# A two-layer decoder trunk on one core: the first conditioning pair on TensorE, later pairs in quarter steps, the gates token-major, the second phase split from its third k-tile on

## The chip, the core and the metric

The kernel runs on one core of one Trainium2 chip. The time is device microseconds for one execution, and the number compared is the median of several executions. TensorE (PE), VectorE (DVE), ScalarE (ACT) and the DMA queue of SyncE (SP) each work through a list of their own, in the order of that list, and wait for each other through semaphores. GpSimd (POOL) only clears a few tiles here.

## What is computed

One sequence of 256 tokens (T) and width 2048 (D, so 16 k-tiles of 128, KT) goes through two layers. All that the change touches lies at the very start of layer 0, before the first half of the mixer is done. Cut to that:

```python
mod = silu(c) @ ada_w[0] + ada_b[0]            # (12288): shift, scale, gate of two sub-layers
h = rms_norm(x, norm1_g[0]) * (1 + scale) + shift
p = h @ w_in                                    # 2048 x 8200
qk_m, v_m, o_m, if_m, q_r, k_r, v_r, g_r = split(p)
gates = 15 * tanh((if_m + gate_b) / 15)         # 8 columns: 4 input gates, 4 forget gates
log_i, log_f = gates[:, :4], log_sigmoid(gates[:, 4:])
# mLSTM: exp(dmat - running max) of cumulated gates weights the 256 x 256 scores of each of 4 heads
```

All data is float32. Most products are made in three float32r passes: weight and activation are each split into a rounded high part and a rest, and high x high, high x rest and rest x high are added.

## The kernel before

The normalised input is turned to feature-major, `xT` (16 tiles of 128 x 256). To become `h`, each k-tile needs its shift and its scale, which are sums over 2048 conditioning inputs. They are made in eight pairs (`pr` 0 to 7, two k-tiles each). A pair reads 4.19 MB of `ada_w` as four quarter tiles `ar` (ring of four). VectorE multiplies and adds 16 slices into `acc0`, which is the fold (L752, L754). `row_sums` turns the accumulator on TensorE (L332) and sums it on ScalarE (L335). Two small VectorE operations give `mod` and `acol` (L765, L767), ScalarE makes `hf` (L772), and `split_to_hs` makes the high part and the rest (L206, L207).

Three phases of the input projection run while the pairs are made, because the weights can't be used before the pair is there:

- First phase (`nb`, `q0b`): k-tiles 0 to 3 (`PART`), for the values and the first query columns, in plain float32 from `raw` (`wplain`, or straight in the loop).
- Second phase (`gbs`, `vbs`): k-tiles 0 to 7 (`HALF`), for the output gate and the last values, in plain float32.
- Third phase (`qk = sums(7)`): all 16 k-tiles for 14 column tiles of queries and keys. K-tiles 0 to 5 are in plain float32 from `hf`; the rest is split. `wload` fetches into `raw`; ScalarE rounds to `wh` (L232), VectorE subtracts to `wl` (L234), and `nmul2` issues three matmuls for each column tile.

After the third phase comes the rest of the first phase's columns (k-tiles 4 to 15, all split), called the V phase here. It reuses the seven PSUM banks of the third phase, so ScalarE first copies them out (`qkr`).

`gates()` stands in the program at k-tile 8 of the third phase. It computes the 8 gate columns with `tmul`, feature-major (8 x 256), turns them, forms cumulated sums, a running maximum over 256 positions in eight doubling steps on VectorE (L899, L900), and four 128 x 384 matrices `E`. All of it uses PSUM bank 3 alone, because the seven others hold the third phase.

A fourth thing runs alongside: `Fill`, which folds 512 KB rows of `ada_w` (tile `ada`, L400, L402) for later sub-layers, two to a k-tile from k-tile 12 on.

The order on each engine is set by a scheduler that takes the program in written order with priorities; the splits carry a raised priority. Slots of the rings (`raw`, `wh`, `wl` of four, `ada` of three, `ar` of four) decide when a transfer may be issued, and SP issues transfers strictly in its order.

Of the kernel before, what the change touches and what calls it, by code (L numbers as in the profile page):

```python
# [94 lines left out]
def tile_trunk(ctx: ExitStack, tc: tile.TileContext, io, out):  # L95
# [522 lines left out]
    def mlp(l, before, fill, norm):  # L618
        with ExitStack() as es:
# [33 lines left out]
            if l == 1:  # L653
# [4 lines left out]
                zp.tile([P, 24], F32, name="pad")  # L658
# [32 lines left out]
    with ExitStack() as es:  # L691
# [24 lines left out]
        early = [load_ar(0, 0), load_ar(0, 1)]  # L716
# [25 lines left out]
        sums_of = {}  # L742

        def cond_sum(pr):

            acc = sums_of[pr] = sp0.tile([P, 2, T], F32, tag="acc0", bufs=3, name="acc0")
            for kq in range(4):
                ar = early.pop(0) if early else load_ar(pr, kq)
                for kr in range(4):
                    cc = cond[:, kq * 4 + kr:kq * 4 + kr + 1]  # L750
                    if kq == 0 and kr == 0:
                        V.tensor_scalar(acc, ar[:, kr], cc, None, op0=OP.mult)  # L752
                    else:
                        V.scalar_tensor_tensor(acc, ar[:, kr], cc, acc, op0=OP.mult, op1=OP.add)  # L754

        def cond_pair(pr):

            if pr not in sums_of:
                cond_sum(pr)
            acc = sums_of.pop(pr)  # L760
            cs = st(4, "adac")
            row_sums(cs, [acc[:, i // 2, (i % 2) * P:(i % 2 + 1) * P] for i in range(4)])
            two_k = slice(2 * pr, 2 * pr + 2)
            mview = mod[0][:, 0:32].rearrange("p (c k) -> p c k", c=2)[:, :, two_k]
            V.tensor_tensor(mview, cs.rearrange("p (c k) -> p c k", c=2),  # L765
                            bada[0][:, 0:32].rearrange("p (c k) -> p c k", c=2)[:, :, two_k], op=OP.add)
            V.scalar_tensor_tensor(acol[:, 0, 0, two_k], mod[0][:, 16 + 2 * pr:18 + 2 * pr], 1.0,  # L767
                                   ngain[0, 0][:, two_k], op0=OP.add, op1=OP.mult)
            out = {}
            for k in (2 * pr, 2 * pr + 1):  # L770
                hf = sp0.tile([P, T], F32, tag="hf", bufs=8, name="hf") if k < HALF else tmp.tile([P, T], F32, tag="half", name="half")
                S.activation(hf, xT[:, k, :], AF.Identity, scale=acol[:, 0, 0, k:k + 1], bias=shift(0, 0)[:, k:k + 1])  # L772
                hs[k] = split_to_hs(hf)
                out[k] = hf
            return out
# [18 lines left out]
        hfs = {}  # L794
        for pr in range(PART // 2):
            ws = {}
            hfs.update(cond_pair(pr))
# [23 lines left out]
        def load_c(k):  # L821
            wc[k] = wplain(k, 3072, 4096), wplain(k, 6664, 7176)

        for k in range(PART):
            load_c(k)
            if k % 2 == 1:
                cond_sum((PART + k - 1) // 2)
        for k in range(HALF):
# [4 lines left out]
            for j in range(8):  # L833
                mm(gbs[j // 2][:, j % 2 * T:j % 2 * T + T], wa[:, j * P:(j + 1) * P], hfs[k], a and j % 2 == 0, z)
            for t in range(2):
                mm(vbs[t], hfs[k][:, t * P:(t + 1) * P], wb[:, 0:512], a, z)
            if k % 2 == 1 and k < PART:
                hfs.update(cond_pair((PART + k - 1) // 2))
            elif k % 2 == 1:
                cond_sum((PART + k - 1) // 2)  # L840
# [12 lines left out]
        c1 = sp0.tile([P, c1w], F32, name="c1")  # L853
# [541 lines left out]
```

## Time and profile before

| | |
|---|---|
| median of 3 runs | 2344.75 us (2341.22 to 2345.06) |
| profiled execution | 2340.88 us |
| its span, first to last instruction | 2339.1 us |
| PE, DVE, ACT busy | 97%, 73%, 51% of the span |
| HBM read | 607 MB, 261 GB/s over the span |

TensorE's idle time is nearly all in the first tenth of the span, and the change is made there. The profile's timeline of one engine gives, for merged instructions, their start, the time that they took together, and in brackets the idle time before them with what ended it. Its groups by shape give the busy time, the mean of one instruction in ns, and the idle time before them.

### The profile page before, as it was taken

The numbers are of one execution on the slowest core, as the hardware profiler recorded it, in microseconds if no ns is written. First come the engines' busy times: TensorE is split into PE (matmuls) and PEld (weight loads), VectorE is DVE, ScalarE is ACT, GpSimd is POOL, SyncE is SP. The second block draws the span as 40 slices with busy tenths as digits, with TensorE's granted clock in tenths as the row PEclk, the third lists the DMA queues.
The fourth block names the chain that finished last, engine by engine and source line by source line (L and its number), as shares of the span: only waits on it lengthen the run. The fifth ranks groups of instructions, "written<-read, shape, count | busy, mean of one in ns | idle before, by whom it ended". The sixth has DMA issues, their size and how long they took to land.

```text
span 2339.1 us, 37507 instructions
## 1 busy us (share of the span) xinstructions
PE 2280.5 (97%) x14121; PEld 2033.0 (87%) x14121; DVE 1704.9 (73%) x2499; ACT 1191.6 (51%) x2248; POOL 0.5 (0%) x8
## 2 busy tenths in 40 slices
PE   5899998999999999999999999999999999999999
PEld 3689888999988888999989899999988888888887
DVE  5768897995877777888988779865777455555555
ACT  3225455455555556655555445664655555444443
POOL 0000000000000000000000000000000000000000
PEclk8999999999999999999999999999999999999999
DMA  9998998996699999999899787645798665555554
GB/s 329 355 300 285 297 319 286 326 325 207 215 311 318 317 316 315 310 305 315 284 327 320 233 271 229 227 139 176 242 313 269 182 188 188 189 198 192 193 191 162
DMA packets 268909, 611.97 MB, mean 262 GB/s; under 512 B 26692, under 2 KB 95286, under 8 KB 268728
## 3 DMA queue, kind: packets, MB, share of 16 engines
q1 hardware_dynamic: 268728, 609.59, 78.2%
q8 instruction: 110, 1.80, 0.3%
q14 instruction: 71, 0.58, 0.1%
HBM read 607.38 MB, written 2.12 MB: 261 GB/s over the span
## 4 chain that ended last, share of the span: by engine, by line
PE 80%; DVE 9%; DMA 6%; issue 2%; ACT 2%; SPq 0%; DVEq 0%; ACTq 0%
PE L L124 49%; PE M L124 30%; DMA ada<-in_ada_w_dram 3%; DVE wl L234 3%; DMA raw<-in_even_w_in_dram 2%; DVE acc L402 1%; DVE acc L754 1%; PE M L332 1%; ACT wh L232 1%; DMA raw<-in_mlp_w_dram 1%; ACT junk L335 0%; DVE cv L1064 0%; DVE hs L207 0%; SPq L243 0%; PE M L737 0%
## 5 line engine op out<-in xcount | busy, mean ns | idle before, releaser
L234 DVE TENSOR_TENSOR wl<-raw,wh 128x1024 fp32r<-128x1024 f32 (+1 forms) x724 | 876.7, 1213 | 489.4 <-ACT wh L232 480.1
L232 ACT CAST wh<-raw 128x1024 fp32r<-128x1024 f32 (+1 forms) x724 | 753.7, 1042 | 830.6 <-PE M L124 442.1
L124 PE MATMUL L<-hs,wh 128*128 128x256 f32 (+1 forms) x4608 | 1131.7, 324 | 6.5 <-ACT wh L232 4.2
L124 PE MATMUL L<-hs,wl 128*128 128x256 f32 x3120 | 874.8, 281 | 2.4 <-DVE wl L234 2.4
L124 PEld LDWEIGHTS L<-hs,wh 128*128 128x128 f32 x4608 | 772.1, 190 | 70.9 <-ACT wh L232 5.9
L124 PEld LDWEIGHTS L<-hs,wl 128*128 128x128 f32 x3120 | 591.0, 190 | 4.1 <-DVE wl L234 3.2
L124 PE MATMUL M<-hs,wh 128*128 128x512 f32 (+2 forms) x1816 | 518.6, 347 | 0.0
L402 DVE SCALAR_TENSOR_TENSOR acc<-ada,cond,acc 128x1024 f32<-128x1024 f32 x300 | 383.3, 1278 | 30.5 <-DMA ada<-in_ada_w_dram 30.0
L124 PE MATMUL M<-hs,wl 128*128 128x256 f32 (+2 forms) x1444 | 403.1, 279 | 0.0
L124 PEld LDWEIGHTS M<-hs,wh 128*128 128x128 f32 (+1 forms) x1816 | 313.7, 187 | 52.1 <-issue 1.6
L124 PEld LDWEIGHTS M<-hs,wl 128*128 128x128 f32 (+2 forms) x1444 | 269.2, 186 | 1.9 <-issue 1.0
L124 PE MATMUL L<-wh,zh 128*128 128x512 f32 x512 | 168.7, 389 | 0.0
L124 PE MATMUL M<-wh,zh 128*128 128x512 f32 x512 | 168.6, 389 | 0.0
L124 PEld LDWEIGHTS L<-wh,zh 128*128 128x128 f32 x512 | 96.0, 188 | 20.2 <-issue 0.3
L124 PEld LDWEIGHTS M<-wh,zh 128*128 128x128 f32 x512 | 96.2, 188 | 20.0
L335 ACT ACTIVATE junk<-M 128x128 f32<-128x128 f32 x210 | 55.2, 278 | 88.0 <-PE M L332 87.9
L124 PE MATMUL L<-wl,zh 128*128 128x512 f32 x256 | 99.7, 389 | 0.0
L124 PE MATMUL M<-wl,zh 128*128 128x512 f32 x256 | 99.6, 389 | 0.0
L754 DVE SCALAR_TENSOR_TENSOR acc<-ar,cond,acc 128x512 f32<-128x512 f32 x120 | 90.2, 751 | 4.8 <-DMA ar<-in_ada_w_dram 1.0
L634 ACT ACTIVATE half<-half 128x256 f32<-128x256 f32 x120 | 47.8, 411 | 28.6 <-DVE half L325 28.6
L124 PE MATMUL L<-hf,raw 128*128 128x256 f32 x224 | 53.3, 392 | 4.9 <-DMA raw<-in_even_w_in_dram 4.9
L124 PEld LDWEIGHTS L<-wl,zh 128*128 128x128 f32 x256 | 48.1, 188 | 10.2 <-DVE wl L234 0.3
(273 smaller groups left out, 1575.4 us busy)
## 6 DMA issues: line engine op xcount, KB each, us to landing
raw<-in_mlp_w_dram SPq DMA_DIRECT2D x504, 512.0 KB, 4.6
ada<-in_ada_w_dram SPq DMA_DIRECT2D x320, 512.0 KB, 5.3
raw<-in_even_w_in_dram SPq DMA_DIRECT2D x136, 256.0 KB, 5.4
ar<-in_ada_w_dram SPq DMA_DIRECT2D x64, 512.0 KB, 7.8
raw<-in_odd_w_in_dram SPq DMA_DIRECT2D x48, 512.0 KB, 4.5
raw<-in_even_w_out_dram SPq DMA_DIRECT2D x32, 512.0 KB, 5.3
raw<-in_odd_w_out_dram SPq DMA_DIRECT2D x32, 512.0 KB, 4.2
raw<-in_even_w_in_dram SPq DMA_DIRECT2D x28, 512.0 KB, 6.1
```

Source lines behind the costliest of these rows:

```text
L124: PE.matmul(o, a, b, start=start, stop=stop, skip_group_check=True)
L232: S.copy(wh[:, :n], raw[:, :n])
L234: last_split[0] = V.tensor_tensor(wl[:, :n], raw[:, :n], wh[:, :n].bitcast(F32), op=OP.subtract)
L332: PE.transpose(b[:, i * P:(i + 1) * P], t, ident)
L335: S.activation(j, b[:, i * P:(i + 1) * P], func, accum_out=dst[:, i:i + 1])
L402: V.scalar_tensor_tensor(acc, r, cond[:, kr:kr + 1], acc, op0=OP.mult, op1=OP.add)
L634: S.activation(a, a, AF.Relu)
L754: V.scalar_tensor_tensor(acc, ar[:, kr], cc, acc, op0=OP.mult, op1=OP.add)
```

## The change

The change has five parts.

1. All four quarter tiles of pair 0 are requested ahead of the small parameter rows. The pair's 16 slices are multiplied on TensorE: the stationary operand is one column of `cond` repeated 32 times (`cond32`), and slice `kr` of each quarter goes to rows 32 x `kr` of a bank. ScalarE copies the bank out, and a column `quad` that has a one in every 32nd row adds the four strips.
2. For every pair, `row_sums` is replaced by four matmuls with `acc` stationary and one column moving; `mod` reads their result in PSUM.
3. `conditioned()` is a generator: the loops of the phases take it forward by quarters of a pair (`cond_steps`) and no longer by whole pairs.
4. The second phase is split from k-tile 2 on, the third from k-tile 4 on.
5. `gates()` is token-major, 64 small float32r matmuls with the activations stationary and 8 or 16 gate columns moving. It is a generator too, begun at k-tile 8 and taken forward by small steps inside the matmul loop from k-tile 12 on. Its constants `c1` now lie in `xT`, and a padding tile shrinks from 24 to 16 columns.

```diff
-        early = [load_ar(0, 0), load_ar(0, 1)]
+        early = [load_ar(0, kq) for kq in range(4)]
...
+        quad = small.tile([P, 1], F32, tag="quad", bufs=1, name="quad")
+        V.reduce_sum(quad, c0[:, 0:128:32], axis=AX.X)
...
+        def cond32(k):
+            return bass.AP(tensor=cond.tensor, offset=cond.offset + k, ap=[list(cond.ap[0]), [0, 32]])
...
+        def conditioned():
+            for pr in range(KT // 2):
+                acc = sp0.tile([P, 2, T], F32, tag="acc0", bufs=3, name="acc0")
+                if pr == 0:
+                    b = bank(3)
+                for kq in range(4):
+                    ar = early.pop(0) if early else load_ar(pr, kq)
+                    for kr in range(4):
+                        cc = cond[:, kq * 4 + kr:kq * 4 + kr + 1]
+                        if pr == 0:
+                            mm(b[32 * kr:32 * kr + 32, :], cond32(kq * 4 + kr),
+                               ar[:, kr].rearrange("p c t -> p (c t)"), kq == 0, kq == 3)
+                        elif kq == 0 and kr == 0:
+                            V.tensor_scalar(acc, ar[:, kr], cc, None, op0=OP.mult)
+                        else:
+                            V.scalar_tensor_tensor(acc, ar[:, kr], cc, acc, op0=OP.mult, op1=OP.add)
+                    if kq < 3:
+                        yield
+                if pr == 0:
+                    S.copy(acc.rearrange("p c t -> p (c t)"), b)
+                cs = bank(3)[:, 0:4]
+                for i in range(4):
+                    mm(cs[:, i:i + 1], acc[:, i // 2, (i % 2) * P:(i % 2 + 1) * P], one1 if pr else quad, i == 0, i == 3)
...
         def load_c(k):
-            wc[k] = wplain(k, 3072, 4096), wplain(k, 6664, 7176)
+            if k < 2:
+                wc[k] = wplain(k, 3072, 4096), wplain(k, 6664, 7176)
+            else:
+                wc[k] = wload(wE, k, 1, [(3072, 4096)]), wload(wE, k, 1, [(6664, 7176)])
...
+                    nmul2(j % 2)(gbs[j // 2], hs[k], *wa, j * P, P, False, z)
...
             if k == 8:
-                SP.dma_start(c1, io["c1"])
-                gates()
+                gsteps = gates()
+                next(gsteps)
...
-                if k < 6:
+                if k < 4:
                     w = wplain(k, c, c + 896)
...
+                    if k >= 12 and j in (2, 5):
+                        next(gsteps, None)
+            cond_steps(2 if k % 3 == 2 else 1)
```

What this does to the lists of the engines shows at three places. In them `acc_N` is the accumulator of a pair, `M` is a bank of the second PSUM pool (numbers tell one use from another), `L` is a bank of the first.

VectorE where the second phase begins, before: the folds of pair 1 (`acc_301`), the pair's end, then pair 2 (`acc_403`) in one piece.

```order
L754 SCALAR_TENSOR_TENSOR acc_301<-ar,cond,acc_301 128x512 x15
L765 TENSOR_TENSOR mod_83<-adac,prm 128x2x2
L767 SCALAR_TENSOR_TENSOR acol<-mod_83,prm 128x2
L207 TENSOR_TENSOR hs<-hf,hs 128x256 x2
L752 TENSOR_SCALAR acc_403<-ar,cond 128x512
L754 SCALAR_TENSOR_TENSOR acc_403<-ar,cond,acc_403 128x512 x15
```

The same place now, with pair 2 as `acc_389`, pair 3 as `acc_469`.

```order
L767 SCALAR_TENSOR_TENSOR acc_389<-ar,cond,acc_389 128x512 x3
L234 TENSOR_TENSOR wl<-raw,wh 128x1024
L234 TENSOR_TENSOR wl<-raw,wh 128x512
L767 SCALAR_TENSOR_TENSOR acc_389<-ar,cond,acc_389 128x512 x4
L234 TENSOR_TENSOR wl<-raw,wh 128x1024
L234 TENSOR_TENSOR wl<-raw,wh 128x512
L767 SCALAR_TENSOR_TENSOR acc_389<-ar,cond,acc_389 128x512 x8
L765 TENSOR_SCALAR acc_469<-ar,cond 128x512
```

Two k-tiles' splits for the second phase now stand between the quarters of pair 2.

ScalarE at the same place now (`v` and `q` are copies out of the first phase's banks; before, no `wh` stood there).

```order
L689 COPY v_220<-L_228 128x2x256
L689 COPY v_222<-L_229 128x2x256
L232 CAST wh_399<-raw_397 128x1024
L232 CAST wh_405<-raw_403 128x512
L689 COPY v_222<-L_230 128x2x256
L689 COPY v_224<-M0_231 128x2x256
```

The first of these splits, which VectorE's `wl` needs, stands behind three copies that wait for the end of the first phase.

TensorE at one of the four matrices `E` (`M3_1163<-mt` is the first), before: in the midst of k-tile 13 and 14 of the third phase.

```order
L124 MATMUL M2_690<-hs_898,wh_1443 128x256
L124 MATMUL M3_1163<-mt_1140,c1_683 128x256
L124 MATMUL M2_690<-hs_898,wh_1443 128x256
L124 MATMUL M2_690<-hs_898,wl_1444 128x256
L124 MATMUL L_684<-hs_903,wh_1476 128x256 x2
L124 MATMUL L_684<-hs_903,wl_1477 128x256
L124 MATMUL L_684<-hs_903,wh_1476 128x256 x2
```

The same matmuls now (`M2_767` is the last column tile of the third phase, `L_1863` the first bank of the V phase).

```order
L124 MATMUL M2_767<-hs_1461,wh_1817 128x256 x2
L124 MATMUL M2_767<-hs_1461,wl_1818 128x256
L124 MATMUL M3_1719<-mt_1659,xT_82 128x256
L124 MATMUL M3_1744<-mt_1659,xT_82 128x256
L124 MATMUL M3_1760<-mt_1659,xT_82 128x256
L124 MATMUL M3_1791<-mt_1659,xT_82 128x256
L953 MATMUL M3_1807<-c0_78,mt_1659 128x4
L124 MATMUL L_1863<-wh_1872,hs_451 128x512
```

All four now stand between the last matmul of the third phase and the first of the V phase, each into the same bank.

VectorE at that place now (`E<-xT,M_...` are the subtractions that empty the bank).

```order
L935 TENSOR_TENSOR mt<-mt 4x192
L234 TENSOR_TENSOR wl<-raw,wh 128x768
L934 COPY mt<-mt 4x128
L935 TENSOR_TENSOR mt<-mt 4x128
L402 SCALAR_TENSOR_TENSOR acc<-ada,cond,acc 128x1024
L945 TENSOR_TENSOR E<-xT,M_1719 128x256
L946 TENSOR_TENSOR E<-xT,M_1719 128x128
L402 SCALAR_TENSOR_TENSOR acc<-ada,cond,acc 128x1024
L945 TENSOR_TENSOR E<-xT,M_1744 128x256
L946 TENSOR_TENSOR E<-xT,M_1744 128x128
L234 TENSOR_TENSOR wl<-raw,wh 128x1024
L945 TENSOR_TENSOR E<-xT,M_1760 128x256
```

Between the pairs of subtractions stands each time a fold or a split for later work. From the output projection of this mixer on, the lists of all engines are the same as before.

## Rows read from the trace of the kernel before

**Rows 1.** Waits of TensorE, 0 to 220 us: total us, times, longest us.

```profile
PE M L332 <- DVE acc L754: 8.7, 3, 4.6
...
PE L L124 <- DMA raw<-in_even_w_in_dram: 4.9, 2, 4.6
PE L L124 <- ACT hf L772: 4.5, 2, 2.3
```

**Rows 2.** Timeline of TensorE at the phases: start us, us, count, idle before.

```profile
50.13 5.40 PE L124 MATMUL L<-raw,hf 128*128 128x512 f32 x8 [2.26 <-ACT hf L772]
...
57.94 3.60 PE L124 MATMUL L<-raw,hf 128*128 128x512 f32 x8
...
63.95 3.62 PE L124 MATMUL L<-hf,raw 128*128 128x256 f32 x16
...
69.12 3.62 PE L124 MATMUL L<-hf,raw 128*128 128x256 f32 x16
...
109.50 0.60 PE L332 MATMUL M<-c,acc 128*128 128x128 f32 x4
...
158.22 0.40 PE L124 MATMUL M<-hs,wh 128*128 128x256 f32 x2
...
158.58 0.40 PE L124 MATMUL M<-hs,wh 128*128 128x256 f32 x2
...
220.86 0.40 PE L124 MATMUL L<-wh,hs 128*128 128x512 f32 x1
```

**Rows 3.** Timeline of TensorE at small matmuls, in two places.

```profile
185.39 0.73 PE L124 MATMUL M<-lfc,c 128*128 128x4 f32 x6
185.98 0.36 PE L124 MATMUL M<-hs,wl 128*128 128x256 f32 x1
...
1367.14 0.92 PE L124 MATMUL M<-ik,iq 64*128 64x256 f32 x8
1367.99 0.50 PE L124 MATMUL L<-hs,wh 128*128 128x256 f32 x2
```

**Rows 4.** Timeline of VectorE at folds: pair 1, and two waits for transfers.

```profile
34.22 0.48 DVE L752 TENSOR_SCALAR acc<-ar,cond 128x512 f32<-128x512 f32 x1
34.73 11.78 DVE L754 SCALAR_TENSOR_TENSOR acc<-ar,cond,acc 128x512 f32<-128x512 f32 x15
...
53.97 0.49 DVE L752 TENSOR_SCALAR acc<-ar,cond 128x512 f32<-128x512 f32 x1 [2.32 <-DMA ar<-in_ada_w_dram]
...
130.18 0.49 DVE L752 TENSOR_SCALAR acc<-ar,cond 128x512 f32<-128x512 f32 x1 [11.35 <-DMA ar<-in_ada_w_dram]
```

**Rows 5.** Transfers, 10 to 130 us: total.

```profile
DMA packets 32831, 42.22 MB, mean 352 GB/s; under 512 B 1547, under 2 KB 28217, under 8 KB 32825
```

**Rows 6.** VectorE's groups by shape, 0 to 221 us: busy us, mean ns, idle before.

```profile
L234 DVE TENSOR_TENSOR wl<-raw,wh 128x896 fp32r<-128x896 f32 x20 | 21.7, 1084 | 7.3 <-ACT wh L232 7.1 <-PE M L124 0.2
L402 DVE SCALAR_TENSOR_TENSOR acc<-ada,cond,acc 128x1024 f32<-128x1024 f32 x11 | 14.1, 1278 | 4.0 <-DMA ada<-in_ada_w_dram 3.8
...
L207 DVE TENSOR_TENSOR hs<-half,hs 128x256 fp32r<-128x256 f32 x8 | 3.1, 421 | 0.2 <-ACT hs L206 0.2
...
L234 DVE TENSOR_TENSOR wl<-raw,wh 128x1024 fp32r<-128x1024 f32 x2 | 2.4, 1217 | 0.0
L912 DVE TENSOR_TENSOR E<-c,M 128x256 f32<-128x256 f32 x4 | 1.7, 420 | 1.0 <-PE M L124 0.9
...
L913 DVE TENSOR_TENSOR E<-c,M 128x128 f32<-128x128 f32 x4 | 1.1, 280 | 0.0
L234 DVE TENSOR_TENSOR wl<-raw,wh 128x768 fp32r<-128x768 f32 x1 | 0.9, 948 | 0.0
...
L900 DVE TENSOR_TENSOR mt<-mt 4x248 f32<-4x248 f32 x1 | 0.4, 397 | 0.0
```

**Rows 7.** ScalarE's groups by shape, 0 to 221 us.

```profile
L689 ACT COPY v<-L 128x512 f32<-128x512 f32 x4 | 2.3, 586 | 8.7 <-PE L L124 8.7
```

**Rows 8.** Waits of SP's queue, 0 to 220 us: total us, times, longest us.

```profile
SPq L243 <- DVE wl L234: 17.5, 10, 3.3
```

More of the change, by code (lines that the diff above doesn't have):

```diff
@@ L657, in mlp @@
                 place[0] = 0
-                zp.tile([P, 24], F32, name="pad")
+                zp.tile([P, 16], F32, name="pad")
                 result(io["mlp_w2"][l],
@@ L740, in tile_trunk @@
         free[:] = [3]
[L742 to L775, printed above, removed]
+        def cond32(k):
+            return bass.AP(tensor=cond.tensor, offset=cond.offset + k, ap=[list(cond.ap[0]), [0, 32]])
@@ new lines, in tile_trunk @@
+        hfs = {}
+        def conditioned():
[21 more added lines that the diff above has]
+                    mm(cs[:, i:i + 1], acc[:, i // 2, (i % 2) * P:(i % 2 + 1) * P], one1 if pr else quad, i == 0, i == 3)
+                two_k = slice(2 * pr, 2 * pr + 2)
+                mview = mod[0][:, 0:32].rearrange("p (c k) -> p c k", c=2)[:, :, two_k]
+                V.tensor_tensor(mview, cs.rearrange("p (c k) -> p c k", c=2),
+                                bada[0][:, 0:32].rearrange("p (c k) -> p c k", c=2)[:, :, two_k], op=OP.add)
+                V.scalar_tensor_tensor(acol[:, 0, 0, two_k], mod[0][:, 16 + 2 * pr:18 + 2 * pr], 1.0,
+                                       ngain[0, 0][:, two_k], op0=OP.add, op1=OP.mult)
+                for k in (2 * pr, 2 * pr + 1):
+                    hf = sp0.tile([P, T], F32, tag="hf", bufs=8, name="hf") if k < HALF else tmp.tile([P, T], F32, tag="half", name="half")
+                    S.activation(hf, xT[:, k, :], AF.Identity, scale=acol[:, 0, 0, k:k + 1], bias=shift(0, 0)[:, k:k + 1])
+                    hs[k] = split_to_hs(hf)
+                    hfs[k] = hf
+                yield
@@ L778, in tile_trunk, with cond_steps @@
+        steps = conditioned()
+        def cond_steps(n):
+            for _ in range(n):
+                next(steps, None)
         HALF = KT // 2
@@ L902, in gates @@
                 d *= 2
-            b = bank()
-            for t in range(2):
-                PE.transpose(b[:, t * 4:t * 4 + 4], m0[:, t * P:(t + 1) * P], ident[0:4, 0:4])
-            V.tensor_tensor(expm.rearrange("p a b -> p (a b)"), b[:, 0:8], bc.rearrange("p a b -> p (a b)"), op=OP.add)
-            S.activation(expm, expm, AF.Exp, scale=-1.0)
+            yield
+            yield
+            yield
             for h in range(4):
@@ L916, in gates @@
                 emat.append(E)
+                yield
+            b = bank()
+            for t in range(2):
+                PE.transpose(b[:, t * 4:t * 4 + 4], m0[:, t * P:(t + 1) * P], ident[0:4, 0:4])
+            V.tensor_tensor(expm.rearrange("p a b -> p (a b)"), b[:, 0:8], bc.rearrange("p a b -> p (a b)"), op=OP.add)
+            S.activation(expm, expm, AF.Exp, scale=-1.0)
         qk = sums(7)
```

74 lines of the change are left out of this document (44 added, 30 removed).

## The prediction

> **What bounds the kernel now.** I first read TensorE's waits up to the V phase. They show who releases it: folds on VectorE, 8.7 us in three waits, the transfers of weights, 4.9 us, and the activation `hf` at a pair's end, 4.5 us [rows 1]. So the start is a chain of conditioning pairs: transfer, fold, pair's end, next k-tile. TensorE's timeline then gives the phases: k-tile 2 of the first phase starts at 50.13, the second phase at 63.95, its last matmul ends near 109.5, and the V phase starts at 220.86 [rows 2]. From there on the lists change little and later not at all, so I forecast the start of the V phase and carry the difference to the end.
>
> Two rates rule the start. Transfers: VectorE waits for an `ar` quarter at 53.97 and at 130.18 [rows 4]. By then the code has asked for 17.0 and 44.0 MB (x and constants 2.3; a pair 4.19, a quarter 1.05; a k-tile of the three phases 0.92, 0.79, 0.92). That is 0.354 MB per us between the two, and the DMA view has 352 GB/s [rows 5]; so a quarter lands at about 5.5 us + MB / 0.352. VectorE: 15 folds take 11.78 us, 0.785 each, so a quarter costs 3.1 and a pair 12.3 [rows 4].
>
> **The change part by part.**
>
> *Less TensorE work.* A plain k-tile of the first phase takes 6.0 us (57.94 to 63.95) and one of the third has as many columns; one of the second takes 5.2 (63.95 to 69.12) [rows 2]. A split column tile of 256 takes 0.36 us (158.22 to 158.58) [rows 2], so a split k-tile takes 14 x 0.36 = 5.0 us in the third phase and 12 x 0.36 = 4.3 in the second. Six k-tiles save 0.9 and two save 1.0: 7 us. Against that stand the gates: 64 small matmuls with a 128-column weight. The nearest row, six of four columns in 0.59 us (185.39 to 185.98) [rows 3], gives 0.1 each, 6.4 us; that is about as much as the 32 wider ones that they replace need, and TensorE waits for VectorE there anyway (steps 5 and 6), which hides it; without that cover it would cost at most their 6.4.
>
> *More VectorE work.* Pair 0 leaves VectorE: -12.3 us. The new splits are six of 1024 columns at 1.22, six of 512 at about 0.68 (by the step from 896 to 1024) and four of 896 at 1.08 [rows 6]: +15.7. Net +3.4 us on the engine that feeds the chain. ScalarE gets about as many roundings and loses the row sums; it isn't full.
>
> *The pair's end.* Row sums took 3.6 us from the last fold (46.5) to the next matmul (50.13) [rows 2, 4]. Now four one-column matmuls, 8 instructions at 0.1, then the same two VectorE operations and one activation: I take 2.2.
>
> *Pair 0 on TensorE.* The parameter rows are now asked for behind four quarters and no longer two. Pair 0's end needs them (`ngain`); four quarters have landed by 5.5 + 6.5 / 0.352 = 24, so they are there before pair 0 is summed. If not, the first matmul slips, which has about 1 us to spare before step 1. The 16 matmuls of 32 x 512 follow the first 16 turns of x, near 19 us. A plain matmul of 512 columns is two instructions of 0.45 (3.60 for eight) [rows 2]. In sequence they need 14 us, and pair 0 ends at about 35. No row has four column strips; the nearest has two halves of the rows: eight instructions of `iq` in 0.85 us (1367.14 to 1367.99) [rows 3], against 1.3 in sequence (four of 256 columns at 0.22, by 3.62 for 16 [rows 2], four of half that). At that overlap they take about 10, with 2 for the clock: pair 0 ends near 31, the first matmul is at about 33 as before, and k-tile 1 ends near 46. The Trainium skill (TensorE: Matmul & The Clock Gate, Part 3: Packing small matmuls — row/col tiling) says that outputs at different 32-row strips run concurrently, 2.38 times faster for three; by it pair 0 would end near 26. No run here shows that form. It hardly matters: pair 1's quarters set the next step. Pair 1 (12.5 MB asked for) lands at 41.0, is folded at 44.1 and ready at 46.3. K-tile 2 starts at 46.3, against 50.13; strips in sequence would add 2 us.
>
> *The sum to the V phase.*
> 1. K-tiles 2 and 3: 12.0, plus 1.8 because after such a wait eight matmuls take 5.40 and not 3.60 [rows 2]: the first phase ends at **60.1** (before: 63.95).
> 2. Now VectorE's list holds the chain up. `wl` of k-tile 2 stands before the second quarter of pair 2; its `wh` stands on ScalarE behind three copies that wait for the first phase's last matmuls, as they do now [rows 7]. So folds stop until 60.1. Then come three quarters 9.3, k-tile 3's splits 1.9, pair 3's folds 12.3, pair 2's end 1.1, and about 2 of waiting for TensorE's small matmuls: 26.6. Pair 3's four small matmuls stand on TensorE right behind the first matmul of k-tile 4: TensorE, through with k-tile 3 near 79, waits 8 us. K-tile 4 goes on at **87.5**.
> 3. K-tiles 4 to 7: 4 x 4.3, plus 1.8 as in step 1: second phase ends at **106.6** (109.5).
> 4. Three plain k-tiles of the third phase 18.0, pair 4's end and a split before the next fold 2.2: **126.8**.
> 5. From here VectorE's list is full: three quarters 9.3, pairs 6 and 7 24.6, 14 splits 15.2, six `hs` 2.5, three pairs' ends and small ones 2.1 [rows 4, 6]: pair 7 is folded at **180.5**. TensorE's work from 106.6, four plain and eight split k-tiles, ends near 172, so it waits.
> 6. Seven `ada` folds 8.9, eight splits 8.7, `hs` and end 1.1, gates' small operations 3.6, waits 3: the last split is done at **205.8**, the third phase 2.5 later.
> 7. The join. Behind that split VectorE still has four scan steps 2.1 (0.4 and a copy each), four splits 4.3, two `ada` folds 2.6, four times 0.42 + 0.28 for `E` [rows 6]: 11.8. All four rounds share one bank, each matmul waits for the subtraction before it, and TensorE has nothing else. Then two exponentials and the first `qkr` copy (0.59) [rows 7] 1.4: **219.0**, plus 1.8 for the clock.
>
> That is 220.8 against 220.86: **no change**. The 15 us gained by the end of the third phase are given back at the join, where before the four rounds stood among the matmuls of k-tiles 13 and 14 and cost TensorE their own time alone.
>
> **The rivals.**
>
> *VectorE's waits don't arise (faster).* The sum holds 2 + 3 us of small waits, put in by hand, and 3 x 1.8 for the clock, all from one row. If most of these don't come, the V phase starts 9 us earlier: 2336. For it: VectorE waited 2.3 and 11.4 us for single quarters before [rows 4], and finer steps can fill such gaps. Against: nearly all that the sum holds is busy time in a list that is worked through in order, which can't shrink.
>
> *Transfers run dry (slower).* SP issues in order. Now a weight tile for k-tile 6 stands behind the split of k-tile 4 (88), with pair 4's quarters behind it; a tile for third-phase k-tile 1 waits for TensorE's k-tile 6 (101). That kind of wait cost SP 17.5 us before [rows 8]. By the landing rule and steps 1 to 3, what was asked for ahead of these has landed at about 60, 86 and 100, and I find 1, 4 and 2.5 us in which nothing is under way, so quarters land at about 12 us + MB / 0.352; pair 7 (57.5 MB) lands at 175 and VectorE reaches it at 174: just hidden. From there each us more delays the end by one: 9 us more, 2354, if every wait is twice as long as I find.
>
> *Pair 0 in sequence* is the change not doing what it says; +2 us, 2347, inside "no change".
>
> **How the numbers follow.** The sum stands against the profiled execution, 2340.88: -0.1, so 2340.8. The median is 3.87 above that execution, so I give 2344.7. About 0.2%, 4.7 us, is what a measurement of this kernel tells from no change. No change 0.42 (it takes the third rival in), faster 0.34, slower 0.24. Own range of the forecast 2340 to 2349. The full range reaches to the first rival and to the second: 2334 to 2354, which leaves out about 0.2.
>
> **What would show it.** Step 1: a matmul of k-tile 2 near 46 and the first phase's end at 60. Step 2: VectorE idle until 60, and a wait of TensorE of about 8 us for a fold near 80 to 88. Step 5: VectorE over 90% busy from 127 to 206. Step 7: TensorE nearly idle for 10 us before the V phase, with four matmuls of `mt` about 2 us apart. Wrong would be a V phase that starts before 214 or after 227, a join under 6 us, or a second phase that ends near 100: then VectorE was not the pace there.

## The result, and the profile after it

The changed kernel takes 2356.45 us in the median of four executions (2351.52 to 2363.0), against 2344.9 for the kernel before on the same chip: a ratio of 1.0055, with a 95% interval of 1.0039 to 1.0071. It is slower, by about 13 us by the ratio (11.6 between the medians), and lies outside the forecast range (2334 to 2354). In the profiled execution (2351.52 us, span 2349.7) the V phase starts at 231.98, where it started at 220.86 before [rows 2]. That is 11.1 us later, and the span is 10.6 us longer, so the loss is complete before the V phase.

TensorE's timeline of the changed kernel (start, time of the merged instructions, and in brackets the idle time before them with what ended it):

```profile
18.70 2.78 PE L124 MATMUL M<-ar,cond 128*32 128x512 f32 x24
22.22 1.06 PE L124 MATMUL M<-ar,cond 128*32 128x512 f32 x8 [0.74 <-DMA ar<-in_ada_w_dram]
...
28.24 1.02 PE L124 MATMUL L<-raw,hf 128*128 128x512 f32 x2
...
47.13 1.87 PE L124 MATMUL M<-c,acc 128*128 128x1 f32 x8 [6.22 <-DVE acc L767]
50.08 6.71 PE L124 MATMUL L<-raw,hf 128*128 128x512 f32 x8 [1.08 <-ACT hf L783]
...
65.21 3.62 PE L124 MATMUL L<-hf,raw 128*128 128x256 f32 x16
...
89.49 0.38 PE L124 MATMUL L<-hs,wh 128*128 128x256 f32 x1 [4.35 <-ACT wh L232]
91.90 1.84 PE L124 MATMUL M<-c,acc 128*128 128x1 f32 x8 [2.02 <-DVE acc L767]
93.60 1.41 PE L124 MATMUL L<-hs,wh 128*128 128x256 f32 x5
...
112.14 3.61 PE L124 MATMUL L<-hf,raw 128*128 128x256 f32 x16
...
188.19 1.02 PE L124 MATMUL M<-c,acc 128*128 128x1 f32 x8 [2.61 <-DVE acc L767]
189.47 4.22 PE L124 MATMUL M<-w,hs 128*128 128x16 f32 x19 [0.26 <-DVE mod L777]
193.54 1.20 PE L124 MATMUL L<-hs,wh 128*128 128x256 f32 x4
194.54 1.06 PE L124 MATMUL M<-w,hs 128*128 128x8 f32 x5
...
198.59 2.74 PE L124 MATMUL M<-w,hs 128*128 128x16 f32 x20
...
202.70 2.29 PE L124 MATMUL M<-w,hs 128*128 128x16 f32 x20
...
223.66 0.67 PE L124 MATMUL M<-mt,xT 4*128 4x256 f32 x2 [0.77 <-DVE mt L935]
...
231.98 0.80 PE L124 MATMUL L<-wh,hs 128*128 128x512 f32 x1 [0.74 <-ACT qkr L1148]
```

The start of the list is near what [rows 2] was before: k-tile 2 starts at 50.08 (50.13), the first phase ends at 65.21 (63.95), the second at 112.14 (109.50). The new thing is the stretch from 188 to 205: `M<-w,hs` are the 64 gate matmuls. The first 24 take 5.1 us (0.21 each), the next 20 take 2.7 and the last 20 take 2.3 (0.11 each); the rest of the stretch is the column tiles between them.

VectorE in the same stretch, and three stretches of all engines (columns: stretch, length, busy time and count of PE, PEld, DVE, ACT, POOL, then granted clock, DMA share, GB/s):

```profile
195.13 1.08 DVE L234 TENSOR_TENSOR wl<-raw,wh 128x896 fp32r<-128x896 f32 x1
205.24 0.17 DVE L906 TENSOR_TENSOR gc<-M,gc 128x16 f32<-128x16 f32 x1 [9.02 <-ACT gc L905]
...
218.83 1.07 DVE L234 TENSOR_TENSOR wl<-raw,wh 128x896 fp32r<-128x896 f32 x1
```

```profile
60.00:120.00 60.00, 53.62 (x288) 45.34 (x287) 39.88 (x58) 20.16 (x33) 0.00 (x0) 0.94 0.87 280
...
190.00:200.00 10.00, 10.00 (x51) 10.00 (x50) 5.77 (x7) 3.11 (x6) 0.00 (x0) 0.52 0.95 354
200.00:210.00 10.00, 10.00 (x87) 10.00 (x88) 4.08 (x7) 4.91 (x9) 0.00 (x0) 1.00 0.07 12
```

The longest wait of SyncE's queue from 185 to 215 us (total us, times, longest us):

```profile
SPq L395 <- DVE acc L402: 16.1, 3, 12.5
```

Read these together. TensorE has just waited 2.61 us for pair 7. From 190 to 200 it runs at a granted clock of 0.52, about the lower of its two levels (1.2 GHz), and its weight loader (PEld) is busy all 10 us: with the activation as the stationary operand, each small matmul has a 128-column weight to load. ScalarE and VectorE stand at the gate sums `gc`, VectorE for 9.02 us. The splits and the folds of `ada` rows (L402) are queued behind that wait. SyncE stands up to 12.5 us at an `ada` transfer whose slot such a fold must free, the weight tiles stand behind it in SyncE's list, and the transfers stop (12 GB/s from 200 to 210).

### The profile page after: what moved, and what is told of

Same layout as the page of the kernel before. It is cut to its first block, busy times and chain, and to the rows that moved or that the text cites. A ratio compares the mean times of both kernels' runs of the same rounds, so it can differ in the third digit from the quotient of the medians.

```text
span 2349.7 us, 37856 instructions
## 1 busy us (share of the span) xinstructions
PE 2288.9 (97%) x14301; PEld 2052.0 (87%) x14301; DVE 1707.6 (73%) x2499; ACT 1194.6 (51%) x2201; POOL 0.5 (0%) x8
## 4 chain that ended last, share of the span: by engine, by line
PE 84%; DVE 8%; DMA 4%; issue 2%; ACT 1%; SPq 0%; DVEq 0%; ACTq 0%
PE L L124 50%; PE M L124 32%; DVE wl L234 2%; DMA ar<-in_ada_w_dram 2%; DMA raw<-in_even_w_in_dram 1%; DVE acc L767 1%; DVE acc L402 1%; DMA ada<-in_ada_w_dram 1%; PE M L332 1%; ACT wh L232 1%; DVE hs L207 0%; SPq L711 0%; DVE cv L1106 0%; DMA raw<-in_even_w_out_dram 0%; DVE sc L1314 0%
## 5 line engine op out<-in xcount | busy, mean ns | idle before, releaser
L234 DVE TENSOR_TENSOR wl<-raw,wh 128x1024 fp32r<-128x1024 f32 (+1 forms) x740 | 892.6, 1209 | 499.9 <-ACT wh L232 490.3
L232 ACT CAST wh<-raw 128x1024 fp32r<-128x1024 f32 (+1 forms) x740 | 766.6, 1038 | 870.1 <-PE M L124 440.2
L124 PE MATMUL L<-hs,wh 128*128 128x256 f32 (+1 forms) x4736 | 1160.0, 324 | 10.9 <-ACT wh L232 10.9
L124 PE MATMUL L<-hs,wl 128*128 128x256 f32 x3184 | 893.7, 282 | 4.6 <-DVE wl L234 4.4
L124 PEld LDWEIGHTS L<-hs,wh 128*128 128x128 f32 x4736 | 795.6, 191 | 76.0 <-ACT wh L232 11.7
L124 PEld LDWEIGHTS L<-hs,wl 128*128 128x128 f32 x3184 | 604.6, 190 | 6.5 <-DVE wl L234 6.0
L124 PE MATMUL M<-hs,wl 128*128 128x256 f32 x1440 | 401.6, 279 | 0.0
L402 DVE SCALAR_TENSOR_TENSOR acc<-ada,cond,acc 128x1024 f32<-128x1024 f32 x300 | 383.4, 1278 | 18.8 <-DMA ada<-in_ada_w_dram 18.4
L124 PEld LDWEIGHTS M<-hs,wl 128*128 128x128 f32 x1440 | 270.0, 188 | 1.0 <-issue 0.7
L767 DVE SCALAR_TENSOR_TENSOR acc<-ar,cond,acc 128x512 f32<-128x512 f32 x105 | 78.9, 751 | 13.5 <-DMA ar<-in_ada_w_dram 10.5
L124 PEld LDWEIGHTS M<-wl,zh 128*128 128x128 f32 x256 | 48.0, 188 | 9.9
```

The lines of the kernel that those rows point to most:

```text
L124: PE.matmul(o, a, b, start=start, stop=stop, skip_group_check=True)
L232: S.copy(wh[:, :n], raw[:, :n])
L234: last_split[0] = V.tensor_tensor(wl[:, :n], raw[:, :n], wh[:, :n].bitcast(F32), op=OP.subtract)
L402: V.scalar_tensor_tensor(acc, r, cond[:, kr:kr + 1], acc, op0=OP.mult, op1=OP.add)
```

## Experiments

All variants but x8 and x11 to x17 start from the changed kernel; those start from the kernel before. Times are medians; ratios are against the kernel before on the same chip, and differences between runs of different chips are taken from ratios. "V" is the start of the V phase in the profiled execution.

| run | median | ratio, interval | V |
|---|---|---|---|
| changed kernel | 2356.45 | 1.0055 [1.0039, 1.0071] | 231.98 |
| x1 second phase plain | 2361.71 | 1.0082 [1.0067, 1.0097] | 242.19 |
| x2 4 of 64 gate matmuls | 2345.67 | 1.0007 [0.9998, 1.0017] | 222.51 |
| x3 both | 2349.40 | 1.0025 [1.0016, 1.0035] | 224.46 |
| x4 gate sum later | 2357.29 | 1.0060 [1.0045, 1.0075] | 231.53 |
| x5 pairs sooner, gates at 8 | 2359.34 | 1.0073 [1.0057, 1.0089] | 232.26 |
| x6 the same, gates at 9 | 2360.90 | 1.0076 [1.0059, 1.0092] | 233.21 |
| x7 gates of before | 2346.89 | 1.0019 [1.0009, 1.0028] | 224.40 |
| x9 gates ahead of pair 7 | 2349.95 | 1.0029 [1.0015, 1.0043] | 229.10 |
| x10 gates of before, at 8 | 2353.52 | 1.0042 [1.0024, 1.0060] | 228.02 |
| x8 before, pair 0 on TensorE | 2344.05 | 1.0009 [1.0000, 1.0019] | 223.10 |
| x11 before, token-major gates | 2355.16 | 1.0042 [1.0028, 1.0056] | 229.42 |
| x12 before, pair 0, small ends | 2351.36 | 1.0031 [1.0017, 1.0046] | 220.53 |
| x13 the same, filler 16 | 2341.97 | 0.9986 [0.9974, 0.9998] | 221.86 |
| x14 before, filler 16 | 2353.35 | 1.0039 [1.0024, 1.0054] | 220.64 |
| x15 x13, second phase split | 2346.99 | 1.0017 [1.0007, 1.0027] | 228.22 |
| x16 x13, third split from 5th | 2341.43 | 0.9997 [0.9987, 1.0008] | 222.37 |
| x17 x13 again | 2342.17 | 1.0001 [0.9992, 1.0010] | 222.64 |

### The transfers or the gates: x1, x2, x3, x4

Two causes stood in the trace: the transfers, which moved less in the second phase (280 GB/s from 60 to 120), and the gates.

x1 undoes the split of the second phase:

```diff
-            if k < 2:      # in load_c and twice in the loop
+            if k < 8:
```

> The changed kernel with one part undone: all eight k-tiles of the second phase plain again, none split. In the changed kernel the transfers moved 36.3 MB by 120 us where the kernel before had 41.3, and the shares 60 to 100 us are low (241 and 285 KB per ns-thousand, before 366 and 334 GB/s), because SyncE stands behind splits on VectorE. Theory D (dry transfers): that deficit of 5 MB, some 14 us at 0.352 MB per us, makes pair 7 late (folded at 188, before 166) and is the loss; with the second phase plain the transfers have 40 MB or more by 120 us, pair 7 is folded before 180, and the time falls by 6 to 12 us, to 2344 to 2350. Theory G (gates): the loss is the 64 gate matmuls, for which VectorE waits 9.0 us at 196 to 205; the second phase doesn't matter: 2353 to 2359, with that wait still there.

x2 leaves 4 of the 64 gate matmuls, those of k-tile 0, so it leaves out most of the gate sums:

```diff
-            for k in range(KT):
+            for k in range(1):
                 for t in range(2):
                     hi = hs[k][:, t * P:(t + 1) * P]
```

> The changed kernel with 4 of the 64 gate matmuls (those of k-tile 0 alone; the gates are then not the sum over all k-tiles). Everything else stands where it stood. TensorE spent 189.5 to 205 on these and the columns between them, at a granted clock of 0.52 from 190 to 200. Theory G: VectorE's wait of 9.0 us for them goes, SyncE issues on, the time falls by 7 to 10 us, to 2346 to 2350. Theory D: what is late at 188 is pair 7, and the splits after it need their 10 us in any case, so the wait comes back at the next tile: falls by 3 us at most, 2353 to 2357.

x3 has both edits, and x4 moves three empty places of the gates' generator ahead of the evacuation:

> Both edits of the two runs before: second phase plain, and 4 of the 64 gate matmuls (the gates are then not the sum over all k-tiles). If both causes are real and lie one behind the other, the gains add: 2338 to 2343. If one holds the other (the wait for the gates only shows because pair 7 is late, or pair 7's lateness is hidden by the gates), it is as fast as the better of the two alone.

```diff
+            yield
+            yield
+            yield
             o = b[:, 0:32].rearrange("p (t c) -> p t c", t=2)
...
             V.tensor_scalar(lfc, gc[:, :, 12:16], -1.0, None, op0=OP.mult)
-            yield
-            yield
-            yield
```

> The changed kernel with the evacuation of the gate sums (the copy on ScalarE, the adds on VectorE and what follows) put three places later in the third phase, where three empty places were behind them, so that the splits of the next weight tiles stand ahead of the wait. Theory G in the form that the wait costs because splits and with them transfers are queued behind it: the 9.0 us of VectorE shrink to 4 or less, the transfers go on between 200 and 210 us (12 GB/s in the changed kernel), and the time falls by 3 to 7 us. In the form that TensorE's time on the 64 matmuls is itself the loss, or under theory D: within 2 us of 2356.

x2 decides. Without 60 small matmuls the kernel can't be told from the kernel before; they cost 0.0048 of the time, 11 us. Its V phase starts 9.5 us sooner, and VectorE no longer waits for the gate sums. TensorE at the gates, VectorE at the gate sums and TensorE at the V phase, of x2:

```profile
188.52 0.95 PE L124 MATMUL M<-w,hs 128*128 128x16 f32 x4 [0.26 <-DVE mod L777]
...
192.34 0.17 DVE L906 TENSOR_TENSOR gc<-M,gc 128x16 f32<-128x16 f32 x1
...
222.51 0.80 PE L124 MATMUL L<-wh,hs 128*128 128x512 f32 x1 [0.74 <-ACT qkr L1148]
```

x1 brings the transfers back (337 GB/s from 60 to 120, before: 358), here the stretch of the kernel before and that of x1:

```profile
60.00:120.00 60.00, 52.55 (x198) 37.68 (x197) 44.55 (x70) 15.31 (x48) 0.00 (x0) 0.94 1.05 358
```

```profile
60.00:120.00 60.00, 56.97 (x226) 42.27 (x225) 38.42 (x58) 12.00 (x22) 0.00 (x0) 0.97 1.01 337
```

x1 is slower than the changed kernel by some 6 us all the same (the intervals just overlap), and pair 7 is folded at 190.3, not sooner than the 188.1 of the changed kernel. x1 also gives TensorE back the work that the split had saved (6 x 0.9 us by the prediction), so it doesn't price the dry transfers alone; but they aren't the loss. Its own loss shows the gates once more; TensorE, VectorE and a stretch of all engines of x1:

```profile
192.32 4.22 PE L124 MATMUL M<-w,hs 128*128 128x16 f32 x19 [0.26 <-DVE mod L777]
...
201.44 4.26 PE L124 MATMUL M<-w,hs 128*128 128x16 f32 x20
...
208.27 4.26 PE L124 MATMUL M<-w,hs 128*128 128x16 f32 x20
...
212.77 0.17 DVE L906 TENSOR_TENSOR gc<-M,gc 128x16 f32<-128x16 f32 x1 [13.71 <-ACT gc L905]
```

```profile
204.00:208.00 4.00, 4.00 (x19) 4.00 (x20) 0.00 (x0) 0.00 (x0) 0.00 (x0) 0.50 0.00 0
```

Here all 64 run at a granted clock of 0.50, 20 in 4.26 us, and VectorE waits 13.71 us; at the end of that wait VectorE, ScalarE and the transfers stand at nothing. x3 against x2 (the intervals just touch) has the split of the second phase worth 4 us in this kernel, once the gates don't hide it: the transfers are back in x3 too (338 GB/s from 60 to 120, against 284 in x2), and it is the slower one. x4 was as slow as the changed kernel, and VectorE waits about as long:

```profile
203.11 0.17 DVE L909 TENSOR_TENSOR gc<-M,gc 128x16 f32<-128x16 f32 x1 [8.82 <-ACT gc L908]
```

The last split ahead of the gate sums is the same as in the changed kernel, so the edit didn't bring the next splits ahead of the wait. Whether the wait would cost less with other work in front of it was therefore not tested.

### Place or form of the gates: x5, x6, x7, x9, x10, x11

x5 and x6 bring the last pair and the gates forward by four or three k-tiles:

```diff
-            cond_steps(2 if k % 3 == 2 else 1)
+            cond_steps(2)
...
-                    if k >= 12 and j in (2, 5):
+                    if k >= 8 and j in (2, 5):      # x6: k >= 9
```

> The changed kernel with two quarter steps behind each k-tile of the third phase (pair 7 ends behind k-tile 7, as before the change, and not behind 11), and the gates' steps from k-tile 8 on, not from 12. Theory P (place): the gates lose because they can't start before the last pair, which the change puts behind k-tile 11: their 64 matmuls meet a TensorE that has just waited and runs at a granted clock of 0.52, and scan and E rounds have four k-tiles to hide in, so 12 us stand alone at the end (219.9 to 231.9). Placed as here they hide: no stretch of 10 us with TensorE busy under 7 before the V phase, the 64 matmuls at 0.11 us each (7 us, full clock), 2336 to 2346. Theory F (form): 64 token-major matmuls are dear wherever they stand: 2348 to 2356. Theory D (transfers): pair 7 can't be folded much before 188, TensorE waits for it ahead of k-tile 8: 2350 to 2360.

> As the run with two quarter steps behind each k-tile of the third phase and gates from k-tile 8, but with the gates' steps from k-tile 9 on, one k-tile (5 us of TensorE) behind the last pair. Theory P: within 3 us of that run, or up to 4 faster if the gates' first matmuls waited there for the last pair's activation. Theory F: as that run. Theory D: up to 5 faster than that run, since TensorE has k-tile 8 to work on meanwhile.

x7 puts `gates()` of the kernel before, as it stood, at the head of k-tile 12 (cut to the call):

```diff
-            if k == 8:
-                gsteps = gates()
-                next(gsteps)
+            if k == 12:
+                gates()      # that of the kernel before, with tmul
```

> The changed kernel with the gates of the kernel before (16 k-tiles in the feature-major form, 32 matmuls of 512 and 256 columns with an 8-column weight, all of the gates' code in one piece) put at the head of k-tile 12, where the changed kernel starts its own. Theory F (the token-major form is what costs): the wait of 9.0 us shrinks, 2346 to 2351. Theory P (the place costs, whatever the form): 2353 to 2360, since the 32 wide matmuls need 16 x 0.33 us at full clock and about twice that at half, and the chain behind them still begins at k-tile 12.

The place is not it. x5 has no join at the end (its four `E` rounds stand between 211 and 219 among columns) and is no faster: its gate matmuls run from 173.74 to 191.0 with the columns between them, and VectorE waits 10.84 us. The form is: x7 has the late place and its join, and is 8 us faster than the changed kernel, with 32 wide matmuls. Its TensorE (first gate matmul, and the first one at full speed) and VectorE at the gate sums:

```profile
186.68 0.59 PE L124 MATMUL M<-hs,wh 128*8 128x512 f32 x1 [1.27 <-ACT wh L232]
...
191.12 0.43 PE L124 MATMUL M<-hs,wh 128*8 128x512 f32 x1
...
194.88 0.41 DVE L325 TENSOR_TENSOR gl<-M,half 8x256 f32<-8x256 f32 x1 [1.52 <-ACT half L324]
```

Theory P falls here.

x11 puts the whole token-major `gates()` into the kernel before, at the place of its own gates, with nothing else changed (cut to the call):

```diff
-                gates()
+                for _ in gates():      # the token-major ones
+                    pass
```

> The kernel before with the token-major gates in the place of its own (at the head of k-tile 8, all steps in one piece), nothing else changed. Theory F: the form costs in this kernel too; TensorE has run full there with short waits (1.5 us), so between 64 x 0.11 - 32 x 0.17 = 1.5 us at full clock and about 8 at half: 2344 to 2351, and a stretch at half clock around 170 to 185 if it is the upper end. If the form costs only in the place that the change gives it: within 2 us of before, 2340 to 2344.

It costs 0.0042, 10 us, more than expected. TensorE of the kernel before at this place (first and last pair of its 32 gate matmuls, and the row where they get faster), then a stretch of all engines:

```profile
169.51 0.63 PE L124 MATMUL M<-hs,wh 128*8 128x512 f32 x1
...
170.75 0.40 PE L124 MATMUL M<-hs,wh 128*8 128x512 f32 x1
...
175.28 0.39 PE L124 MATMUL M<-hs,wh 128*8 128x512 f32 x1
```

```profile
172.00:176.00 4.00, 4.00 (x26) 2.25 (x25) 1.23 (x2) 0.29 (x1) 0.00 (x0) 1.00 0.89 292
```

And of x11, TensorE and VectorE, then the stretches:

```profile
169.72 11.94 PE L124 MATMUL M<-w,hs 128*128 128x16 f32 x56
...
185.10 0.17 DVE L882 TENSOR_TENSOR gc<-M,gc 128x16 f32<-128x16 f32 x1 [12.32 <-ACT gc L881]
```

```profile
172.00:176.00 4.00, 4.00 (x21) 4.00 (x20) 0.78 (x1) 0.00 (x0) 0.00 (x0) 0.50 0.82 280
...
180.00:184.00 4.00, 4.00 (x20) 4.00 (x20) 0.00 (x0) 0.00 (x0) 0.00 (x0) 0.50 0.00 0
```

Both start within 0.2 us of each other, after a wait of 1.5 to 1.6 us for pair 7, one of 0.5 to 0.8 for a split, and ten or eleven column matmuls. The wide ones take 6.1 us and are at full speed from the fifth on (0.63, then 0.40 us). The small ones take 11.94 us for 56, 0.213 each, and the clock stays at 0.50 until the columns come; the weight loader is busy 4.00 of 4.00, against 2.25.

x9 keeps the small form, but sums k-tiles 0 to 13 ahead of pair 7's end, in the bank that pair 7's sums then share:

```diff
+                if pr == 7:
+                    next(gsteps_[0])             # 56 gate matmuls
+                    cs = gbank[0][:, 64:68]
...
-                if k in (5, 10):
+                if k in (13, 14):
```

> The changed kernel with 56 of the 64 gate matmuls (k-tiles 0 to 13) ahead of pair 7's end and 8 behind it; pair 7's four sums use free columns of the same bank. Theory F, as it now stands: in the changed kernel the 64 matmuls are on the path, between pair 7's end (188.2) and the gate sums (205.2), 5.1 us for the first 24 at half clock, 2.6 and 2.2 for the next 20s, 9.8 in all, and the rise of the clock comes late. Ahead of pair 7's end TensorE waits 2.6 us anyway, and has run columns until then: 56 at 0.11 are 6.2, of which 2.6 are free, and 8 remain behind: 4 to 7 us faster, 2349 to 2353, and VectorE's wait for the gate sums under 4 us. Theory S (the number alone: every one costs TensorE its time wherever it stands, since TensorE has no idle time to lose there): within 2 us of 2356.

TensorE and VectorE of x9:

```profile
186.81 3.97 PE L124 MATMUL M<-w,hs 128*128 128x8 f32 x35
...
199.51 0.17 DVE L911 TENSOR_TENSOR gc<-M,gc 128x16 f32<-128x16 f32 x1 [2.50 <-ACT gc L910]
```

Ahead of the wait 35 take 3.97 us, 0.113 each; VectorE's wait falls from 9.02 to 2.50, and the kernel gains 6 us, as expected (the intervals just overlap). So the price hangs on both: how many stand behind the last pair, and at which clock.

x10 has the gates of before at k-tile 8 and the faster pairs of x5:

> The changed kernel with the gates of the kernel before at the head of k-tile 8 (as there) and two quarter steps behind each k-tile of the third phase, so that pair 7 ends behind k-tile 7. Against the run with token-major gates at this place (2359) theory F gives what the form cost there: 64 matmuls from 173.7 to 190.8, granted clock 0.56, against about 7 us for the 32 wide ones: 8 to 11 us faster, 2348 to 2351. If also the place pays, once the form doesn't cost (E rounds among columns, no join of 7 to 12 us), it comes out below the 2346.9 of the gates of before at k-tile 12: 2338 to 2345. If VectorE's folds hold it up there as much as the join did: 2345 to 2351.

Against x5 (the same place, small form) it gains 0.0031, 7 us, by intervals that just overlap: the form again, somewhat less than expected. Against x7 it loses 0.0023 (the intervals overlap), so the earlier place buys nothing.

### The other parts: x8, x12 to x17

x8 and x12 try pair 0 on TensorE, and then the small ends, in the kernel before:

> The kernel before with one part of the change alone: pair 0 summed on TensorE in four column strips (all four quarters asked for ahead), its row sums taken as before with a scale of 1/32. In the changed kernel pair 0 is done at 23.3 and the first matmul stands at 28.2 (before 32.8), but k-tile 2 starts at 50.08 as before (50.13), because pair 1's quarters set it. If transfers alone set the start: within 2 us of before, 2341 to 2345. If VectorE's 12.3 us that become free shorten the later waits of TensorE for folds (8.7 us before): 3 to 7 us faster, 2336 to 2340. Slower only if four quarters ahead of the first weights delay k-tile 0: up to 2347.

```diff
-            row_sums(cs, [acc[:, i // 2, ...] for i in range(4)])
+            cs = bank(3)[:, 0:4]
+            for i in range(4):
+                mm(cs[:, i:i + 1], acc[:, i // 2, ...], one1 if pr else quad, i == 0, i == 3)
```

> The kernel before with pair 0 on TensorE and the pairs' ends as four one-column matmuls (no transposes, no row sums on ScalarE), all else as before the change. Pair 0 alone came out at 2344, no gain. A pair's end measured 3.0 us in the changed kernel (last fold 47.07, k-tile 2 at 50.08) and 3.6 before; 0.6 each for three or four pairs that TensorE waits for: 2 us at most. Expected 2340 to 2344; a time under 2339 would mean that the row sums on ScalarE held more than their own 0.6.

Pair 0 on TensorE alone changes nothing that stands clear of the noise: the first matmul comes 5 us sooner, and k-tile 2 starts at 50.42, as before. x12 was 7 us slower, though its V phase starts at 220.53. The loss is behind 1988 us, in the last stage. Groups by shape of the last stage, from 2000 to 2330 us (busy us, mean ns of one), of the kernel before, x12 and x14 in this order:

```profile
L124 PE MATMUL M<-wh,zh 128*128 128x512 f32 x487 | 160.1, 389 | 0.0
```

```profile
L124 PE MATMUL M<-wh,zh 128*128 128x512 f32 x472 | 157.9, 396 | 0.0
```

```profile
L124 PE MATMUL M<-wh,zh 128*128 128x512 f32 x472 | 157.8, 395 | 0.0
```

The same matmul takes 6 to 7 ns more, and the stage has 1536 of them. A filler tile named `pad` stands ahead of the buffers `zh`; the change makes it 16 columns wide and not 24. x13 and x14 separate that:

```diff
-                zp.tile([P, 24], F32, name="pad")
+                zp.tile([P, 16], F32, name="pad")
```

> The kernel before with pair 0 on TensorE and small ends, as the run that came out at 2351, with one more edit: the filler tile of the last stage has 16 columns, as in the changed kernel, and not 24. That run reached the V phase at 220.5 like the kernel before, and lost 9.7 us from 1988 on, where TensorE never waits and a matmul of the last stage takes 396 ns in the mean and not 389. Theory A (address): its new column tile moves the buffers of the last stage by a few bytes, and the filler sets them right again: 2339 to 2344, last stage 350.7 us from the last gelu row to the end. Theory B (something of the pairs' ends itself): 2349 to 2353.

> The kernel before with nothing changed but the filler tile of the last stage, 16 columns and not 24. Theory A: the buffers stand wrong now, the last stage takes 9 to 10 us more, 2350 to 2354, all of it behind 1988 us. Theory B: within 2 us of before.

The filler alone makes the kernel before 9 us slower, and makes x12 7 to 10 us faster (x17 and x13): by this reading the new column tile had moved the buffers, and the edit moves them back. In the changed kernel the stage is as long as before (from the last `half` at 1999.03 to the end 350.7 us; before, from 1988.28, 350.8), so the filler belongs to the change and costs or gains it nothing. x13 came out just below the kernel before, and x17 is the same kernel with more executions:

> The kernel that came out at 2342 against 2344.8 (ratio 0.9986, interval 0.9974 to 0.9998) once more, in more rounds. If pair 0 on TensorE and small ends gain what the pairs' ends measured (0.6 us for each of three or four ends that TensorE waits for): 0.9985 to 0.9995. If the first time was chance: 0.9995 to 1.0010.

The ratio is 1.0001: no gain. x15 and x16 add one split each to x13:

```diff
# x15, in load_c and in the loop, as in the change
-            wc[k] = wplain(k, 3072, 4096), wplain(k, 6664, 7176)
+            if k >= 2: wc[k] = wload(wE, k, 1, [(3072, 4096)]), wload(wE, k, 1, [(6664, 7176)])
# x16
-                if k < 6:
+                if k < 4:
```

> The kernel that came out at 2342 (before with pair 0 on TensorE, small ends, filler of 16 columns) with the second phase split from its third k-tile on, as the change has it, and nothing else. By the prediction's terms: TensorE saves 6 x 0.9 us, VectorE gets six splits of 1024 and six of 512 columns, 11.4 us, in a stretch in which TensorE waits for its folds. If TensorE's work sets the time: 2337 to 2341. If VectorE's folds and SyncE behind them do: 2345 to 2352. In the changed kernel without its gate matmuls the split was worth 3.7 us (2345.7 against 2349.4).

> The same kernel (2342) with the third phase split from its fifth k-tile on and not from its seventh, as the change has it, and nothing else. TensorE saves 2 x 1.0 us, VectorE gets four splits of 896 columns, 4.3 us, between 130 and 160, where it waits 11 us for a quarter: 2339 to 2342 if that wait takes them in; 2344 to 2348 if they push the folds of pairs 6 and 7, for which TensorE waits at 162.

The split of the third phase from its fifth k-tile on costs nothing. The split of the second costs 0.0016 here, 4 us against x17 on the same chip (the intervals just overlap), and TensorE waits for splits; the first line of its waits up to the V phase (us, times, longest):

```profile
PE L L124 <- ACT wh L232: 11.2, 2, 7.9
```

In the changed kernel, with quarter steps and without the gate matmuls, the same split gained 4 us (x2 against x3). Whether the quarter steps are what turns the sign wasn't tried. No version tried beats the kernel before.

## Why the prediction was wrong, point by point

| point | forecast | measured | late by |
|---|---|---|---|
| k-tile 2 starts | 46.3 | 50.08 | 3.8 |
| step 1, first phase ends | 60.1 | 65.2 | 5.1 |
| step 2, k-tile 4 goes on | 87.5 | 93.6 | 6.1 |
| step 3, second phase ends | 106.6 | 112.1 | 5.5 |
| step 4, pair 4 ended | 126.8 | 132.4 | 5.6 |
| step 5, pair 7 folded | 180.5 | 188.1 | 7.6 |
| step 6, last split done | 205.8 | 219.9 | 14.1 |
| step 7, V phase, without the 1.8 for the clock | 219.0 | 232.0 | 13.0 |

**The step that failed is the price of the gates**, in "Less TensorE work": 64 matmuls at 0.1 each, hidden because "TensorE waits for VectorE there anyway", and step 6 with 3.6 us for the gates' operations and 3 for waits. Step 6 took 31.8 us and not 25.3; in x2, with 4 of the 64, it took 25.0 (pair 7 folded at 187.1, the last split done at 212.1). Three things were wrong in it.

- The cover. TensorE waits for pair 7's folds, and all 64 stand behind that wait in its list, so they can't fill it. Only the 8 of k-tiles 14 and 15 need pair 7; the other 56 stood behind the wait because the program put them there, and x9, which moves them ahead, gained 6 us. The text looked at how long TensorE waits, and not at where the gate matmuls stand and what they need.
- The price. [rows 3] gave 0.1, and that holds at full clock (0.11 in the last 20). Right behind a wait it is 0.21. The prediction put 1.8 us for the clock at three other waits, and nothing here.
- Who waits. The prediction named nobody for the gate sums. VectorE stood there for 9.0 us and ScalarE for 10.3, with splits and folds behind them and the transfers behind those.

With 60 of these matmuls taken out (x2) the ratio is 1.0007, which on the first chip would be 2346.5, 1.8 above the forecast: the rest of the change is, as forecast, no change. That it lies so near is partly luck. In x2 too pair 7 is folded 6.6 us later than forecast; the join then took 10.5 us and not 13.2, and the V phase starts at 222.5, 3.5 late. Of the 13.0 us in the last row, 9.5 go with the gate matmuls, and the rest is what steps 1 to 5 had too short, less what step 7 had too long.

**Step 1 was 3.8 us late.** Pair 1's second quarter is folded from 37.66, behind a wait for its transfer, where the landing rule put it at 35; from there 12 folds run to 47.07:

```profile
37.66 9.41 DVE L767 SCALAR_TENSOR_TENSOR acc<-ar,cond,acc 128x512 f32<-128x512 f32 x12 [1.14 <-DMA ar<-in_ada_w_dram]
...
65.28 3.11 DVE L767 SCALAR_TENSOR_TENSOR acc<-ar,cond,acc 128x512 f32<-128x512 f32 x4
```

That is 3.0 of the 3.8. A pair's end took 3.0 us and not 2.2, since its eight small matmuls take 1.87 at a TensorE that has waited; this 0.8 is the same mistake in small, a row of the full clock used behind a wait. After that the steps kept their lengths within 2 us each until step 6.

**Step 2 and step 7 were right in what they describe.** VectorE did stop folding until the first phase's end (folds from 65.28, the row above), and TensorE stood until pair 3 was folded: 6.4 us and not 8, of which the first 4.35 are put down to a split (`wh`) whose weight tile came late (ScalarE waited 6.45 us for it), and the last 2.02 to the fold. The terms of step 2 add up to 86.7 and not to 87.5, which changes nothing here. The join took 12 us (219.9 to 232.0), forecast 13.2, with the four matmuls of `mt` one by one.

**The rivals.** "Transfers run dry" named what is seen (SyncE in order behind splits, 280 GB/s where 358 stood), and gave 2354, the nearest of the three. But it isn't the cause: x1 brought the transfers back without a gain, and so did x3, set against x2. It would be easy to take the low rates for proof. "VectorE's waits don't arise" did not come. "Pair 0 in sequence" did not either: 24 strips took 2.78 us, 0.12 each, against 0.45 for a plain one [rows 2], so four strips do run side by side. The Trainium skill (TensorE: Matmul & The Clock Gate, Part 3: Packing small matmuls — row/col tiling) says that such strips run concurrently, and the prediction's estimate by its figure had pair 0 end near 26. It ended near 25, and the trace agrees. As the prediction said, it hardly mattered.

## What to carry to other kernels

Before you call work hidden in an engine's wait, ask whether it stands ahead of the wait in that engine's list, and whether it needs the very thing the engine waits for. Work behind the wait isn't hidden, it is the next link of the chain; if most of it doesn't need what the wait is for, move that part ahead (x9). Price small matmuls from rows with the same weight and at the clock of their place, not by the columns they move; here the form with the short side stationary was the cheaper one behind a wait (x7 and x11). When a variant loses time, look for the stretch where it is lost before you explain it: the 7 us of x12 had nothing to do with its edit's place in the program.

## What the runs showed of the hardware

- Behind a wait, 56 small matmuls in a row ran at 0.213 us each, granted clock 0.50 from 170 to 184 us with TensorE busy throughout (x11). The 32 wide ones at the same place were at full speed 1.2 us after their start (before), and in x7 4.4 us after it (from 186.68 to 191.1). In x9, right behind columns at full clock, 35 small ones took 0.113 each.
- A filler tile eight columns narrower ahead of the moving operand's buffers changed a 512-column matmul from 389 to 395 ns, without any wait, for 9 us over the last stage (x14). That it is the place of the buffers is read from the edit; which places are good wasn't tried further.
- Four column strips of 32 took 0.12 us for each 512-column instruction (24 in 2.78 us, the changed kernel), a quarter of the 0.45 of a plain one.
